# Rotary embedding on one core: batch 0 in four parts, a fixed ring order, tables on ScalarE's queue

## Chip, cores and metric

The kernel runs on one core of a Trainium2 chip. The metric is the device time of one execution in microseconds (us), as the median of several runs. A core has five engines with an instruction stream each. Here VectorE (DVE) does the arithmetic, ScalarE (ACT) changes types, GpSimd (POOL) and SyncE (SP) issue DMA transfers, and TensorE (PE) does nothing. The transfers themselves are carried out by sixteen DMA engines, which serve all queues.

## The reference

```python
# x: (8, 2048, 16, 64) float32; cos, sin: (2048, 32) float32
x1 = x[..., :32]
x2 = x[..., 32:]
cos = cos[None, :, None, :]
sin = sin[None, :, None, :]
out1 = x1 * cos - x2 * sin
out2 = x1 * sin + x2 * cos
return np.concatenate([out1, out2], axis=-1)   # float32
```

Each of 8 batches has 2048 positions with 16 heads of 64 values. The two halves of a head are rotated against each other by the position's angle. A batch is 8.39 MB (8 MiB) in float32; all of x is read once and all of out is written once, 67.1 MB each way.

## The kernel before

**Tiling.** The 2048 positions of a batch lie on the 128 partitions, 16 successive positions on each (J = 16; the text calls them rows, index j). So a partition holds one run of 64 KB of x per batch. On the chip a batch is a float16 tile `xt` of 128 x 16384 values; a pool holds five of them (NBUF = 5). POOL's transfers change the type on the way: a load (L51) reads float32 and writes float16, a store (L58) does the reverse. SP's transfers don't change the type, so what SP moves goes through the float32 tile `head` (two rows) and is changed by ScalarE.

**Start.** SP issues three transfers, one behind the other on its queue: rows 0 to 2 of batch 0 into `head` (L36), the sine table (L45) and the cosine table (L46), 256 KB each. POOL issues the loads of batches 0 to 4, batch 0 without its first two rows. ScalarE turns `head` into the first rows of tile 0 (L75), and the tables into float16: `sin_h` (L79), `neg_h`, which is minus sine (L80), and `cos_h` (L81).

**A batch.** `rotate` is four VectorE instructions on a whole tile: v's first halves are x2 times `neg_h` (L67), v's second halves are x1 times `sin_h` (L68), xt is multiplied by `cos_h` in place (L70), and v is added to xt (L72). L67 and L68 take 8192 elements per partition, L70 and L72 take 16384. Then the tile is stored. When tile b has been stored, its buffer takes the load of batch b + 5.

**Order.** Each engine works through its own instructions in order, and POOL's transfers run in the order in which they were issued (the ring). A tile scheduler may move instructions of an engine; POOL's order came out as loads 0 to 4, stores 0 and 1, loads 5 and 6, stores 2 and 3, load 7, stores 4 to 6, then the two parts of the last store. A load into a used buffer waits until the store out of it has landed.

**End.** Batch 7 is stored in three parts: rows 0 to 9 (L95) and 9 to 14 (L97) by POOL, in this order by a dependency written out by hand; rows 14 to 16 are widened to float32 by ScalarE into `head` (L105) and sent by SP (L106), which waits, again by hand, until the part of L95 has landed.

Of the kernel before, what the change touches and what calls it, by code (L numbers as in the profile page):

```python
# [1 line left out]

# [4 lines left out]


@with_exitstack  # L10
def kernel(
    ctx: ExitStack,
    tc: tile.TileContext,
    x: bass.AP,
    cos: bass.AP,
    sin: bass.AP,
    out: bass.AP,
):
    nc = tc.nc
    f16 = mybir.dt.float16  # L20
    f32 = mybir.dt.float32

    B, S, H, D = x.shape
    Dh = D // 2
    P = nc.NUM_PARTITIONS
    J = S // P
    NBUF = 5

    const_pool = ctx.enter_context(tc.tile_pool(name="rope_const", bufs=1))
    io_pool = ctx.enter_context(tc.tile_pool(name="rope_io", bufs=NBUF))  # L30
    tmp_pool = ctx.enter_context(tc.tile_pool(name="rope_tmp", bufs=1))

    JA = 2
    head = const_pool.tile([P, JA, H, D], f32)
    x0 = x[0].rearrange("(p j) h d -> p j (h d)", j=J)
    nc.sync.dma_start(  # L36
        out=head.rearrange("p j h d -> p (j h d)"),
        in_=x0[:, 0:JA, :].rearrange("p j f -> p (j f)"),
    )
    sin_f = const_pool.tile([P, J, Dh], f32)  # L40
    cos_f = const_pool.tile([P, J, Dh], f32)
    cos_h = const_pool.tile([P, J, Dh], f16)
    sin_h = const_pool.tile([P, J, Dh], f16)
    neg_h = const_pool.tile([P, J, Dh], f16)
    nc.sync.dma_start(out=sin_f, in_=sin.rearrange("(p j) d -> p j d", j=J))  # L45
    nc.sync.dma_start(out=cos_f, in_=cos.rearrange("(p j) d -> p j d", j=J))  # L46

    def load(b):
        xt = io_pool.tile([P, J, H, D], f16)
        j0 = JA if b == 0 else 0  # L50
        nc.gpsimd.dma_start(  # L51
            out=xt[:, j0:J, :, :].rearrange("p j h d -> p (j h d)"),
            in_=x[b].rearrange("(p j) h d -> p j (h d)", j=J)[:, j0:J, :].rearrange("p j f -> p (j f)"),
        )
        return xt

    def store(b, xt):
        nc.gpsimd.dma_start(  # L58
            out=out[b].rearrange("(p j) h d -> p (j h d)", j=J), in_=xt
        )  # L60

    def rotate(xt):
        v = tmp_pool.tile([P, J, H, D], f16)
        sin_b = sin_h.unsqueeze(2).to_broadcast([P, J, H, Dh])
        neg_b = neg_h.unsqueeze(2).to_broadcast([P, J, H, Dh])
        cos_b = cos_h.unsqueeze(2).to_broadcast([P, J, 2 * H, Dh])
        nc.vector.tensor_mul(out=v[:, :, :, 0:Dh], in0=xt[:, :, :, Dh:D], in1=neg_b)  # L67
        nc.vector.tensor_mul(out=v[:, :, :, Dh:D], in0=xt[:, :, :, 0:Dh], in1=sin_b)  # L68
        xw = xt.rearrange("p j h (e d) -> p j (h e) d", d=Dh)
        nc.vector.tensor_mul(out=xw, in0=xw, in1=cos_b)  # L70
        xa = xt.rearrange("p j h d -> p (j h d)")
        nc.vector.tensor_add(out=xa, in0=xa, in1=v.rearrange("p j h d -> p (j h d)"))  # L72

    tiles = [load(b) for b in range(NBUF)]
    nc.scalar.copy(  # L75
        out=tiles[0][:, 0:JA, :, :].rearrange("p j h d -> p (j h d)"),
        in_=head.rearrange("p j h d -> p (j h d)"),
    )
    nc.scalar.copy(out=sin_h, in_=sin_f)  # L79
    nc.scalar.mul(out=neg_h, in_=sin_f, mul=-1.0)  # L80
    nc.scalar.copy(out=cos_h, in_=cos_f)  # L81
    def part(b, j0, j1):
        return (
            out[b].rearrange("(p j) h d -> p j (h d)", j=J)[:, j0:j1, :].rearrange("p j f -> p (j f)"),
            tiles[b][:, j0:j1, :, :].rearrange("p j h d -> p (j h d)"),
        )

    for b in range(B):
        rotate(tiles[b])
        if b < B - 1:  # L90
            store(b, tiles[b])
        if b + NBUF < B:
            tiles.append(load(b + NBUF))
    dst, src = part(B - 1, 0, 9)
    gate = nc.gpsimd.dma_start(out=dst, in_=src)  # L95
    dst, src = part(B - 1, 9, J - JA)
    rest = nc.gpsimd.dma_start(out=dst, in_=src)  # L97
    tc.add_manual_dep(
        rest.ins,
        gate.ins.name,  # L100
        mybir.DependencyInfo(mybir.DependencyClass.NoSync, mybir.DependencyReason.DATA),
        reason="order of the ring",
    )
    dst, src = part(B - 1, J - JA, J)
    nc.scalar.copy(out=head.rearrange("p j h d -> p (j h d)"), in_=src)  # L105
    end = nc.sync.dma_start(out=dst, in_=head.rearrange("p j h d -> p (j h d)"))  # L106
    tc.add_manual_dep(
        end.ins,
        gate.ins.name,
        mybir.DependencyInfo(mybir.DependencyClass.Sync, mybir.DependencyReason.DATA),  # L110
        reason="the last rows go out behind this part",
    )


# [1 line left out]
_INS = ['x', 'cos', 'sin']  # L116
_OUTS = [((8, 2048, 16, 64), 'float32')]


# [23 lines left out]
```

## Time and profile before

| what | value |
|---|---|
| median of 3 runs | 317.42 us (317.40 to 317.48) |
| the profiled execution, its own time | 317.42 us |
| its span (first to last instruction in the trace) | 315.6 us |
| VectorE | 32 instructions |
| `rotate` of one batch, four instructions | 4.43 + 4.42 + 8.69 + 8.69 us |
| ScalarE | 6 instructions, 6.8 us |
| POOL, one DMA issue | 0.53 to 0.67 us of POOL's time |
| load 0 from issue to landing | 22.2 us |
| sin, cos from issue to landing | 15.2 us, 33.9 us |
| `head` in, from issue to landing | 4.7 us |
| `head` out, from issue to landing | 8.4 us |
| first VectorE instruction | starts at 23.51 us |
| last VectorE instruction | starts at 254.99 us, 8.69 us long |

How to read it: all times count from the start of the span. The time of a DMA issue on POOL's or SP's stream is the time of issuing, not of moving data; a landing is the semaphore that tells that all data have arrived. "DMA share" is the mean busy share of the sixteen DMA engines in a stretch; packets are counted where they are recorded, so a short stretch can show a share over 1. The bytes of a transfer that changes type are counted in the type of its destination, so a load of x at full pace shows about half the GB/s of a store.

### The profile page before, as it was taken

Reading aid. Unit: us, or ns where it says so; the run is one execution under the profiler, and the core shown is the slowest. Engines: PE = TensorE matmul, PEld = TensorE weight load, DVE = VectorE, ACT = ScalarE, POOL = GpSimd, SP = SyncE. Lnnn points to the kernel's source line nnn. Section 1 sums busy time; section 2 is a strip of 40 time slices with the busy share of each in tenths; the row PEclk is TensorE's granted clock in tenths of the full one; section 3 lists DMA queues with packets and bytes.
Section 4 is the critical chain, followed back from the end, with each engine's and each line's share of the span. In section 5 each row is a group of like instructions: output and inputs, shape, how many; then the busy total and the mean of one; then the engine's idle time right before and its main releaser. Section 6 shows DMA issues by size and latency. Waiting matters only on the chain.

```text
span 315.6 us, 126 instructions
## 1 busy us (share of the span) xinstructions
DVE 209.2 (66%) x32; ACT 6.8 (2%) x6; POOL 9.4 (3%) x21
## 2 busy tenths in 40 slices
DVE  0009599999999999999979999990009994000000
ACT  4010000000000000000000000000000002000000
POOL 3000000000000000010000000100000001000000
DMA  9899999999999999999999999999999999999998
GB/s 278 184 261 207 200 249 216 199 199 249 216 199 266 399 424 507 399 332 233 233 199 199 390 407 399 399 532 266 199 224 507 399 399 498 432 399 399 432 424 341
DMA packets 3024, 101.71 MB, mean 322 GB/s; under 512 B 336, under 2 KB 336, under 8 KB 592
## 3 DMA queue, kind: packets, MB, share of 16 engines
q0 software_dynamic: 2448, 99.09, 98.0%
q1 hardware_dynamic: 576, 2.62, 2.2%
HBM read 67.63 MB, written 67.11 MB: 427 GB/s over the span
## 4 chain that ended last, share of the span: by engine, by line
issue 25%; DMA 23%; DVE 21%; another core or an unknown queue 13%; POOL 1%; ACT 1%; SPq 0%; POOLq 0%; DVEq 0%; ACTq 0%
DMA xt<-in_x_dram 12%; DMA cos_f<-in_cos_dram 11%; DVE xt L70 8%; DVE xt L72 8%; DVE v L68 3%; DVE v L67 1%; ACT head L105 1%; POOL out_dram L58 1%; POOL xt L51 0%; ACT cos_h L81 0%; SPq L45 0%; SPq L36 0%; POOLq L58 0%; DVEq L67 0%
## 5 line engine op out<-in xcount | busy, mean ns | idle before, releaser
L70 DVE TENSOR_TENSOR xt<-xt,cos_h 128x16384 f16<-128x16384 f16 x8 | 69.5, 8692 | 4.2 <-ACT cos_h L81 3.9
L72 DVE TENSOR_TENSOR xt<-xt,v 128x16384 f16<-128x16384 f16 x8 | 69.5, 8692 | 0.3
L67 DVE TENSOR_TENSOR v<-xt,neg_h 128x8192 f16<-128x8192 f16 x8 | 35.4, 4425 | 50.1 <-DMA xt<-in_x_dram 49.9
L68 DVE TENSOR_TENSOR v<-xt,sin_h 128x8192 f16<-128x8192 f16 x8 | 35.3, 4417 | 0.0
L51 POOL DMA_DIRECT2D xt<-in_x_dram x8 | 4.4, 560 | 117.1 <-DMA out_dram<-xt 116.3
L105 ACT CAST head<-xt 128x2048 f32<-128x2048 f16 x1 | 1.9, 1897 | 227.6 <-DVE xt L72 227.6
L58 POOL DMA_DIRECT2D out_dram<-xt x7 | 3.7, 535 | 87.8 <-DVE xt L72 87.8
L95 POOL DMA_DIRECT2D out_dram<-xt x1 | 0.5, 531 | 50.5 <-DVE xt L72 50.5
L75 ACT CAST xt<-head 128x2048 f16<-128x2048 f32 x1 | 1.9, 1898 | 3.4 <-DMA head<-in_x_dram 3.4
L75 ACT ACT_TABLE_LOAD x1 | 1.3, 1283 | 0.7 <-PEq L127 0.7
L81 ACT CAST cos_h<-cos_f 128x512 f16<-128x512 f32 x1 | 0.6, 617 | 18.0 <-DMA cos_f<-in_cos_dram 18.0
L79 ACT CAST sin_h<-sin_f 128x512 f16<-128x512 f32 x1 | 0.6, 617 | 9.1 <-DMA sin_f<-in_sin_dram 9.1
L80 ACT ACTIVATE neg_h<-sin_f 128x512 f16<-128x512 f32 x1 | 0.6, 624 | 0.0
L97 POOL DMA_DIRECT2D out_dram<-xt x1 | 0.5, 531 | 0.0
L127 POOL MEMSET const-float32-0.0<- 128x1 f32 x1 | 0.1, 98 | 0.2 <-issue 0.2
L127 POOL MEMSET const-bfloat16-1.0<- 128x1 bf16 x1 | 0.1, 101 | 0.0
L127 POOL MEMSET const-float32-1.0<- 128x1 f32 x1 | 0.1, 98 | 0.0
L127 POOL MEMSET const-uint8-127<- 128x1 uint8 x1 | 0.1, 98 | 0.0
## 6 DMA issues: line engine op xcount, KB each, us to landing
xt<-in_x_dram POOLq DMA_DIRECT2D x7, 4096.0 KB, 41.1
out_dram<-xt POOLq DMA_DIRECT2D x1, 4608.0 KB, 42.3
xt<-in_x_dram POOLq DMA_DIRECT2D x1, 3584.0 KB, 22.2
out_dram<-xt POOLq DMA_DIRECT2D x1, 2560.0 KB, 47.9
head<-in_x_dram SPq DMA_DIRECT2D x1, 1024.0 KB, 4.7
out_dram<-head SPq DMA_DIRECT2D x1, 1024.0 KB, 8.4
sin_f<-in_sin_dram SPq DMA_DIRECT2D x1, 256.0 KB, 15.2
cos_f<-in_cos_dram SPq DMA_DIRECT2D x1, 256.0 KB, 33.9
```

Of the source, the lines that this page charges most:

```text
L51: nc.gpsimd.dma_start(out=xt[:, j0:J, :, :].rearrange("p j h d -> p (j h d)"), in_=x[b].rearrange("(p j) h d -> p j (h d)", j=J)[:, j0:J, ...
L58: nc.gpsimd.dma_start(out=out[b].rearrange("(p j) h d -> p (j h d)", j=J), in_=xt)
L67: nc.vector.tensor_mul(out=v[:, :, :, 0:Dh], in0=xt[:, :, :, Dh:D], in1=neg_b)
L68: nc.vector.tensor_mul(out=v[:, :, :, Dh:D], in0=xt[:, :, :, 0:Dh], in1=sin_b)
L70: nc.vector.tensor_mul(out=xw, in0=xw, in1=cos_b)
L72: nc.vector.tensor_add(out=xa, in0=xa, in1=v.rearrange("p j h d -> p (j h d)"))
L75: nc.scalar.copy(out=tiles[0][:, 0:JA, :, :].rearrange("p j h d -> p (j h d)"), in_=head.rearrange("p j h d -> p (j h d)"),)
L79: nc.scalar.copy(out=sin_h, in_=sin_f)
L80: nc.scalar.mul(out=neg_h, in_=sin_f, mul=-1.0)
L81: nc.scalar.copy(out=cos_h, in_=cos_f)
L95: gate = nc.gpsimd.dma_start(out=dst, in_=src)
L105: nc.scalar.copy(out=head.rearrange("p j h d -> p (j h d)"), in_=src)
```

## The change

The two rows of the last batch no longer take their own way; batch 7 is stored whole by POOL. Instead batch 0 is cut at rows 2, 6 and 10. Its first two rows still come through `head`, and its other rows are loaded in three POOL transfers; each of the four parts is rotated by four VectorE instructions of its own and stored when done, the first part through ScalarE, `head` and SP, the others by POOL. The sine and cosine tables are issued from ScalarE's queue rather than from SP's. Every POOL transfer of the ring is tied to the one before it, so that POOL issues them in the order in which they are written: load 0 in three parts, store of rows 2 to 6, store of rows 6 to 10, load 1, store of rows 10 to 16, loads 2 and 3, store 1, load 4, store 2, load 5, and so on, with load 7 behind store 4 and stores 5, 6 and 7 at the end. In the built program ScalarE first issues the two tables, then makes `sin_h` and `neg_h`, then the first rows of tile 0, then `cos_h`, then widens the rotated first rows. VectorE has 44 instructions on data in place of 32.

```diff
-    nc.sync.dma_start(out=head..., in_=x0[:, 0:JA, :]...)
...
-    nc.sync.dma_start(out=sin_f, in_=sin.rearrange("(p j) d -> p j d", j=J))
-    nc.sync.dma_start(out=cos_f, in_=cos.rearrange("(p j) d -> p j d", j=J))
+    cuts = [JA, 6, 10, J]
...
+    nc.sync.dma_start(out=flat(head), in_=rows(x, 0, 0, JA))
+    nc.scalar.dma_start(out=sin_f, in_=sin.rearrange("(p j) d -> p j d", j=J))
+    nc.scalar.dma_start(out=cos_f, in_=cos.rearrange("(p j) d -> p j d", j=J))
+
+    last = []
+
+    def ring(dma):
+        if last:
+            tc.add_manual_dep(
+                dma.ins,
+                last[-1].ins.name,
+                mybir.DependencyInfo(mybir.DependencyClass.NoSync, mybir.DependencyReason.DATA),
+                reason="order of the ring",
+            )
+        last.append(dma)
+
+    def load(b, j0, j1):
+        ring(nc.gpsimd.dma_start(out=flat(tiles[b][:, j0:j1, :, :]), in_=rows(x, b, j0, j1)))
+
+    def store(b, j0, j1):
+        ring(nc.gpsimd.dma_start(out=rows(out, b, j0, j1), in_=flat(tiles[b][:, j0:j1, :, :])))
+
+    def rotate(b, j0, j1):
+        xt = tiles[b]
+        n = j1 - j0
+        js = slice(j0, j1)
+        vt = tmp_pool.tile([P, J, H, D], f16)
+        v = vt[:, 0:n, :, :]
...
+        nc.vector.tensor_mul(out=v[:, :, :, 0:Dh], in0=xt[:, js, :, Dh:D], in1=neg_b)
+        nc.vector.tensor_mul(out=v[:, :, :, Dh:D], in0=xt[:, js, :, 0:Dh], in1=sin_b)
+        xw = xt[:, js, :, :].rearrange("p j h (e d) -> p j (h e) d", d=Dh)
+        nc.vector.tensor_mul(out=xw, in0=xw, in1=cos_b)
+        xa = flat(xt[:, js, :, :])
+        nc.vector.tensor_add(out=xa, in0=xa, in1=flat(v))
...
+    fresh(0)
+    for j0, j1 in zip(cuts, cuts[1:]):
+        load(0, j0, j1)
+    nc.scalar.copy(out=flat(tiles[0][:, 0:JA, :, :]), in_=flat(head))
     nc.scalar.copy(out=sin_h, in_=sin_f)
     nc.scalar.mul(out=neg_h, in_=sin_f, mul=-1.0)
     nc.scalar.copy(out=cos_h, in_=cos_f)
...
-    for b in range(B):
-        rotate(tiles[b])
-        if b < B - 1:
-            store(b, tiles[b])
-        if b + NBUF < B:
-            tiles.append(load(b + NBUF))
...
-    nc.scalar.copy(out=head.rearrange("p j h d -> p (j h d)"), in_=src)
-    end = nc.sync.dma_start(out=dst, in_=head.rearrange("p j h d -> p (j h d)"))
...
+    rotate(0, 0, JA)
+    nc.scalar.copy(out=flat(head), in_=flat(tiles[0][:, 0:JA, :, :]))
+    nc.sync.dma_start(out=rows(out, 0, 0, JA), in_=flat(head))
+    rotate(0, cuts[0], cuts[1])
+    store(0, cuts[0], cuts[1])
+    rotate(0, cuts[1], cuts[2])
+    store(0, cuts[1], cuts[2])
+    fresh(1)
+    load(1, 0, J)
+    rotate(0, cuts[2], cuts[3])
+    store(0, cuts[2], cuts[3])
+    fresh(2)
+    load(2, 0, J)
+    fresh(3)
+    load(3, 0, J)
+    for b in range(1, B):
+        rotate(b, 0, J)
+        store(b, 0, J)
+        if b + 3 < B:
+            fresh(b + 3)
+            load(b + 3, 0, J)
```

`fresh(b)` takes a new tile from the pool of five for batch b; `rows` and `flat` are the access patterns of a transfer's two sides, as before.

More of the change, by code (lines that the diff above doesn't have):

```diff
@@ L33 @@
     JA = 2
[L34 to L39, printed above, removed]
+    cuts = [JA, 6, 10, J]
     sin_f = const_pool.tile([P, J, Dh], f32)
@@ L44 @@
     neg_h = const_pool.tile([P, J, Dh], f16)
-    nc.sync.dma_start(out=sin_f, in_=sin.rearrange("(p j) d -> p j d", j=J))
-    nc.sync.dma_start(out=cos_f, in_=cos.rearrange("(p j) d -> p j d", j=J))
-    def load(b):
-        xt = io_pool.tile([P, J, H, D], f16)
[L50 to L78, printed above, removed]
+    head = const_pool.tile([P, JA, H, D], f32)
+    def flat(t):
+        return t.rearrange("p j h d -> p (j h d)")
+    def rows(t, b, j0, j1):
+        return t[b].rearrange("(p j) h d -> p j (h d)", j=J)[:, j0:j1, :].rearrange("p j f -> p (j f)")
+    nc.sync.dma_start(out=flat(head), in_=rows(x, 0, 0, JA))
@@ new lines, in store @@
+    def store(b, j0, j1):
[6 more added lines that the diff above has]
+        v = vt[:, 0:n, :, :]
+        sin_b = sin_h[:, js, :].unsqueeze(2).to_broadcast([P, n, H, Dh])
+        neg_b = neg_h[:, js, :].unsqueeze(2).to_broadcast([P, n, H, Dh])
+        cos_b = cos_h[:, js, :].unsqueeze(2).to_broadcast([P, n, 2 * H, Dh])
+        nc.vector.tensor_mul(out=v[:, :, :, 0:Dh], in0=xt[:, js, :, Dh:D], in1=neg_b)
[4 more added lines that the diff above has]
+        nc.vector.tensor_add(out=xa, in0=xa, in1=flat(v))
@@ L79, with fresh @@
+    tiles = {}
+    def fresh(b):
+        xt = io_pool.tile([P, J, H, D], f16)
+        tiles[b] = xt
+    fresh(0)
+    for j0, j1 in zip(cuts, cuts[1:]):
+        load(0, j0, j1)
+    nc.scalar.copy(out=flat(tiles[0][:, 0:JA, :, :]), in_=flat(head))
     nc.scalar.copy(out=sin_h, in_=sin_f)
@@ L81 @@
     nc.scalar.copy(out=cos_h, in_=cos_f)
[L82 to L86, printed above, removed]
-    for b in range(B):
-        rotate(tiles[b])
-        if b < B - 1:
-            store(b, tiles[b])
-        if b + NBUF < B:
-            tiles.append(load(b + NBUF))
[L94 to L104, printed above, removed]
-    nc.scalar.copy(out=head.rearrange("p j h d -> p (j h d)"), in_=src)
[L106 to L112, printed above, removed]
+    rotate(0, 0, JA)
[19 more added lines that the diff above has]
+            load(b + 3, 0, J)
 _INS = ['x', 'cos', 'sin']
```

## The prediction, made before the changed kernel was run

> **What bounds the kernel now.** I read the page's busy table and its forty slices first, then its DMA queues, then stretches of the span, then the instructions in order of time. Page, engines and queues:
>
> ```profile
> span 315.6 us, 126 instructions
> DVE 209.2 (66%) x32; ACT 6.8 (2%) x6; POOL 9.4 (3%) x21
> ...
> DMA  9899999999999999999999999999999999999998
> ...
> DMA packets 3024, 101.71 MB, mean 322 GB/s; under 512 B 336, under 2 KB 336, under 8 KB 592
> q0 software_dynamic: 2448, 99.09, 98.0%
> q1 hardware_dynamic: 576, 2.62, 2.2%
> HBM read 67.63 MB, written 67.11 MB: 427 GB/s over the span
> ```
>
> VectorE works for two thirds of the span; the sixteen DMA engines never fall below eight tenths, and the POOL queue (q0) alone fills 98.0%. So the DMA engines are the bound, and a change is worth what it does to their idle time, nothing else. The packet counts say how a transfer looks: 2448 = 17 POOL transfers x (128 + 16), so one packet for each partition row, eight on each engine, and one completion packet per engine; q1 likewise is 4 x 144.
>
> In order of time (start, duration, instruction), only the starting and ending lines and those of POOL that were held back by a store:
>
> ```profile
> 0.74 0.38 SPq L36 DMA_DIRECT2D head<-in_x_dram  x1
> 1.17 0.43 SPq L45 DMA_DIRECT2D sin_f<-in_sin_dram  x1
> 1.25 2.79 POOL L51 DMA_DIRECT2D xt<-in_x_dram  x5 [0.80 <-PEq L138]
> ...
> 5.45 1.90 ACT L75 CAST xt<-head 128x2048 f16<-128x2048 f32 x1 [3.43 <-DMA head<-in_x_dram]
> 16.41 0.62 ACT L79 CAST sin_h<-sin_f 128x512 f16<-128x512 f32 x1 [9.07 <-DMA sin_f<-in_sin_dram]
> ...
> 23.51 4.43 DVE L67 TENSOR_TENSOR v<-xt,neg_h 128x8192 f16<-128x8192 f16 x1 [23.51 <-DMA xt<-in_x_dram]
> ...
> 35.55 0.62 ACT L81 CAST cos_h<-cos_f 128x512 f16<-128x512 f32 x1 [17.98 <-DMA cos_f<-in_cos_dram]
> ...
> 54.18 0.54 POOL L58 DMA_DIRECT2D out_dram<-xt  x1 [50.14 <-DVE xt L72]
> ...
> 121.83 0.53 POOL L51 DMA_DIRECT2D xt<-in_x_dram  x1 [41.14 <-DMA out_dram<-xt]
> ...
> 141.13 0.53 POOL L51 DMA_DIRECT2D xt<-in_x_dram  x1 [18.76 <-DMA out_dram<-xt]
> ...
> 306.36 0.35 SPq L106 DMA_DIRECT2D out_dram<-head  x1
> ```
>
> Three things are to be seen. The stores of batches 0 and 1 landed 19.30 us apart (121.83 to 141.13): that is the pace of one batch on a full ring, 1.21 us for each of the 16 rows per partition (j), and 2.41 us for one 64 KB packet. The cosine table, 256 KB, landed at 35.5; batch 0 could not be finished before, and its store was issued at 54.18. Nobody paid for that: five loads were queued at the start and kept the ring full to about 102 (121.8 less one store). All this cover is what the new order gives up.
>
> **The change, part by part.** The time before is one execution: span 315.65 us (three decimals 315.649), its run 317.42, so 1.77 lies around the span; 317.42 is also the median of the three runs.
>
> *Ring order.* POOL now issues: batch 0 in three loads (rows 2 to 6, 6 to 10, 10 to 16; I call them La, Lb, Lc), store of rows 2 to 6 (Sa), store of rows 6 to 10 (Sb), load 1, store of rows 10 to 16, loads 2 and 3, and from there store b, load b+3. Sa waits for VectorE, and since the order is fixed, Sb, load 1 and everything else stands behind that wait. Loads 1 to 4 no longer cover the start: the ring holds 14/16 of a batch, the head, the tables and the small SP store until Sa, and nothing after Sa until Sb.
>
> *When the tables come.* sin landed at 16.4 and cos 19.1 us later, while POOL packets of 2.13 us (batch 0, 14 rows: 14/16 x 2.43) and 2.43 us ran; eight rows and a completion in 19.1 us is 2.12 us each. So while the ring is busy one small packet gets through for each big one. La and Lb have packets of four rows, 4 x 0.151 = 0.60 us. The head takes eight packets of 0.31 us per engine, the trace's packet records say, from 1.74; sin, now on a queue of its own, alternates with it (0.08 us each), so when POOL's first packet comes, at 5.10 in those records, some seven of eight are through on the slowest engine. Left are one sin packet and its completion, eight of cos and its completion: 11 turns of 0.60 + 0.09 = 7.6, so 12.7, and with the landing 12.9 for the start of the ACT cast. Bounds: 11 (one or two turns saved by completion packets, or HW packets passing together) and 15 (POOL's first packet at 3 to 4 instead of 5.1, as three issues now end at 3.0 where five ended at 4.04: every earlier POOL packet takes a turn from head and sin).
>
> The Trainium skill speaks against the queue move: "DMA: Bandwidth & Descriptors", section "Issuing engines are not separate DMA queues", says that transfers issued from several engines run on the same sixteen engines and that only issue time is saved. The row above does show one pool being shared; with the tables behind the head on SP's queue the count of turns after 5.1 would be the same 11 or so, so by the rule and by the row cos comes near 13: what shortens its wait is the size of the load packets.
>
> *VectorE's chain to Sb.* cast of cos 0.62 (L81's duration). A batch takes 26.24 us (53.65 to 79.89); the durations 4.424 for 8192 and 8.692 for 16384 elements give 1.92 elements per ns and about 0.64 us of start costs per batch, so 2 rows take 3.8, of which the last two instructions, after cos, 2.5; 4 rows take 25.6/4 + 0.64 = 7.04; 6 rows 10.2. Rows 0 to 2 end at 12.9 + 0.65 + 2.5 = 16.05, rows 2 to 6 at 23.1, rows 6 to 10 at 30.1. POOL starts 0.28 to 0.57 later (the gaps at 80.15 and 54.18), so Sa is issued at 23.5, Sb at 30.5, load 1 half a microsecond later. The ScalarE cast of rows 0 to 2 (1.90) ends at 18.0 and SP sends them at once.
>
> *What the DMA engines have until then.* Head, tables and batch 0 are through at about 23.5 (VectorE started on batch 0 at 23.51 before, four cos packets of 0.1 still open). The SP store adds 2.41, so 25.9; Sa adds 4 x 1.21 = 4.83, so 30.7. Beyond this the engines stand idle until Sb's first packet: 30.5 + latency.
>
> *Latency from a POOL issue to its first packet on an empty ring.* The trace has it once: issue at 1.25, first packet at 5.10, 3.85 us, cold and with four more issues behind it, and these stretches agree (columns: stretch, length, busy times, clock, DMA share, GB/s):
>
> ```profile
> 0.00:1.50 1.50, 0.00 (x0) 0.76 (x1) 0.46 (x5) 1.00 0.00 0
> 1.50:2.50 1.00, 0.00 (x0) 0.52 (x1) 1.00 (x3) 1.00 0.78 156
> 2.50:5.00 2.50, 0.00 (x0) 0.00 (x0) 1.54 (x3) 1.00 0.95 392
> ...
> 311.50:314.50 3.00, 0.00 (x0) 0.00 (x0) 0.00 (x0) 1.00 0.85 350
> 314.50:315.60 1.10, 0.00 (x0) 0.00 (x0) 0.00 (x0) 1.00 0.00 0
> ```
>
> 156 x 1.0 + 392 x 2.5 is 1.14 MB by 5.0: the head (1.05) and some sin, no load. The other end is SP's 1.0 us (issue 0.74, first packet 1.74); from the end of the fifth issue at 4.04 to 5.10 is also 1.06. I take 2.2, between the two readings of POOL's own row. Idle: 30.5 + 2.2 - 30.7 = **2.0 us**, from 0 (11 for cos, 1.0) to 5.7 (15, 3.85).
>
> The Trainium skill, "DMA: Bandwidth & Descriptors", section "Specifications", gives the first byte of the POOL path as about 1 us; by it the idle time would be 0.8 and the run near 317.9. No run here shows that figure on a warm queue.
>
> *Later waits.* VectorE needs 26.2 per batch, the ring 38.6 per load and store. Load 1 ends near 57, so store 1 is issued near 83 while loads 2 and 3 run to about 103; load 7 ends near 258, store 7 is issued near 284 while stores 5 and 6 run to 296. Load b+3 waits for store b-2, two transfers back. Cost nothing; without that cover a late store would cost what it is late.
>
> *Reads in a row.* Five loads, head and tables before took from 1.74 to about 101.9. At pace they are 5 x 19.3 (head included) + 1.4 of tables = 97.9, +0.45 for slow first packets; 1.2 us over is spread on loads 3 and 4 (packets of 2.5, and 3.3 for the last), while load and store pace elsewhere is 19.3. The new order has at most two loads in a row. If the row of five causes it, it goes; if it is the first touch of the output, most of it stays: -0.6, from -1.2 to 0.
>
> *The end.* The two rows that SP sent (eight packets of 0.31 = 2.47) go back into store 7 (2.41): nothing. A POOL landing is told about 0.2 us later than an SP landing (0.4 to 0.6 after the last packet against 0.3 to 0.4): +0.2. Three more transfers, 0.03 us each by the parts of the last store (10.89 for 9/16, at pace 10.86): +0.1. The removed ScalarE cast was hidden under stores.
>
> Sum: 2.0 - 0.6 + 0.3 = +1.7: span 317.35, time **319.1**.
>
> **The rivals.**
> 1. *The ring never runs dry.* If cos start plus latency is at most 13.1 (12.1 and 1.0, say), Sb arrives before Sa is done. Then -0.6 + 0.3 is left: 317.1, from 316.5 to 317.7. For it: the 1.06 us row, and the small packets; against it: VectorE needs 7.04 for a part that the DMA engines store in 4.83.
> 2. *Starved harder.* Latency 3.85 on every dry issue and cos at 15 give 5.7 + 0.3 - 0.6: 322.8; from 321.1 to 325. For it the only POOL row; against, that row is the first of the program.
> 3. *The tables come no sooner.* If POOL packets shut them out until batch 0 is loaded, cos comes at 23.5, 10.6 later: near 330. Against: sin and cos did get through, one per packet.
>
> **How the numbers follow.** Forecast 58% (idle 0.9 to 4.0: 318.1 to 321.1), rival 1 25%, rival 2 12%, rival 3 5%. 0.2% (0.63 us) is about what a measurement of this kernel can tell from no change: slower than 318.05 is 0.58 + 0.12 + 0.05 = 0.75. Rival 1 straddles 316.79: 0.15 within, 0.10 faster. The range leaves out about a tenth on each side: 316.8 to 321.8; the likeliest case's own is 318.1 to 321.1.
>
> **What would show it.** Cos cast at 11 to 15; POOL's Sa near 23.5 and Sb near 30.5, both released by VectorE; DMA shares well under 0.9 somewhere between 25 and 34, worth about 2 us, and none after; store 7 issued more than 10 us ahead of its turn. I am wrong if no stretch around 30 is below 0.9 (rival 1), if cos comes after 16, or if later stretches lose DMA time.

## The result and the profile after

The changed kernel takes 318.76 us (median of 6 runs, 318.42 to 319.39), the kernel before in the same comparison 317.45 us. The ratio is 1.0042, with a 95% interval of 1.0029 to 1.0055: slower by 1.3 us. The profiled execution took 318.73 us with a span of 316.95 (before: 317.42 and 315.65), so it shows the whole difference.

Page of the changed kernel, engines, slices and queues:

```profile
span 317.0 us, 145 instructions
DVE 210.8 (67%) x44; ACT 6.7 (2%) x6; POOL 11.1 (3%) x24
...
DMA  7999999999999999999999999999999999999996
...
q0 software_dynamic: 2880, 99.09, 97.8%
q1 hardware_dynamic: 288, 2.10, 1.8%
q10 hardware_dynamic: 288, 0.52, 0.5%
```

The tables have a queue of their own (q10). The slices that matter are not where the forecast looked: a dry ring around 30 us would lie in the fourth slice, and that is a 9. The last slice fell, from 8 to 6. The first fell too, from 9 to 7, but that is counting: a packet counts where its record stands, and the kernel before, with packets of 2.13 us at that place, shows a share of 1.37 for 5 to 10 us (1.06 now, with packets of 0.62), while 0 to 5 us show 0.63 and 0.64.

Instructions of the changed kernel in order of time:

```profile
7.22 0.62 ACT L96 CAST sin_h<-sin_f 128x512 f16<-128x512 f32 x1 [4.29 <-DMA sin_f<-in_sin_dram]
...
12.65 0.62 ACT L98 CAST cos_h<-cos_f 128x512 f16<-128x512 f32 x1 [2.49 <-DMA cos_f<-in_cos_dram]
...
23.12 0.54 POOL L68 DMA_DIRECT2D out_dram<-xt  x1 [20.14 <-DVE xt L84]
...
30.17 0.54 POOL L68 DMA_DIRECT2D out_dram<-xt  x1 [6.50 <-DVE xt L84]
30.69 0.54 POOL L65 DMA_DIRECT2D xt<-in_x_dram  x1
...
283.65 0.53 POOL L68 DMA_DIRECT2D out_dram<-xt  x1 [38.13 <-DVE xt L84]
```

The cosine cast at 12.65 and the stores Sa and Sb at 23.12 and 30.17 are within 0.4 us of the working (12.9, 23.5, 30.5), and store 7 was issued at 283.65 (284). So VectorE's chain is as worked out. But no DMA time was lost on Sb: in the trace's packet records Sa's last packets on the sixteen engines end from 31.39 to 32.04, and Sb's first packet starts at 31.39. The stretches agree:

```profile
27.00:31.00 4.00, 3.93 (x3) 0.00 (x0) 0.83 (x2) 1.00 1.09 446
31.00:32.00 1.00, 1.00 (x2) 0.00 (x0) 0.23 (x1) 1.00 0.95 377
32.00:37.00 5.00, 4.93 (x3) 0.00 (x0) 0.00 (x0) 1.00 1.40 475
```

The ring never ran dry there. From load 1 on, every transfer starts 19.32 us per batch after the one before it, to the end. Counted to the last data packet the changed kernel is only 0.25 us behind, 314.68 against 314.43.

The rest lies behind the last packet. There each engine drains (a DRAIN is an instruction that ends when the engine's own work is through, as VectorE's of 8725 ns does beside its last instruction of 8.69 us) and then takes part in the closing barrier, semaphores by which the engines tell one another that they are done. Two answers about the program's last line, first the kernel before, then the changed kernel (columns: engine's queue, operation, count, duration in ns as least/median/most, first and last start in us; POOL's longest drain is the one that starts first):

```profile
L138 POOLq EVENT_SEMAPHORE  x4: 17/17/17, 315.0 to 315.5; - x4
L138 POOLq DRAIN  x3: 39/95/48711, 264.4 to 315.4; - x3
...
L138 DVEq DRAIN  x2: 19/4372/8725, 255.0 to 315.2; - x2
```

```profile
L145 POOLq EVENT_SEMAPHORE  x4: 17/17/17, 315.9 to 316.8; - x4
L145 POOLq DRAIN  x3: 39/95/32267, 283.6 to 316.4; - x3
...
L145 DVEq DRAIN  x2: 143/4434/8725, 274.7 to 316.6; - x2
```

Before, POOL's drain ended at 264.4 + 48.7 = 313.1, while SP's last transfer was still running; that transfer landed at 314.78 (its last semaphore step in the trace) and POOL opened the closing barrier at 314.96, 0.17 later. In the changed kernel store 7 landed at 315.04, but POOL's drain ended only at 283.63 + 32.27 = 315.90 and the barrier opened at 315.94: 0.90 after the landing, so 0.73 us more. POOL's drain was as late before (its own last landing was at 312.35, the drain over 0.74 later, 0.86 in the changed kernel); SP's transfer ran meanwhile. Then VectorE's last drain came late (143 ns in place of 19, started at 316.59): from the barrier to the end it took 1.01 us in place of 0.69. The sum is 0.25 + 0.73 + 0.32 = 1.30 us, the difference of the spans.

### The profile page after: what moved, and what is told of

It is laid out like the page before. It is cut to its first block, busy times and chain, and to the rows that moved or that the text cites. A ratio compares the mean times of both kernels' runs of the same rounds, so it can differ in the third digit from the quotient of the medians.

```text
span 317.0 us, 145 instructions
## 1 busy us (share of the span) xinstructions
DVE 210.8 (67%) x44; ACT 6.7 (2%) x6; POOL 11.1 (3%) x24
## 5 line engine op out<-in xcount | busy, mean ns | idle before, releaser
L79 DVE TENSOR_TENSOR vt<-xt,neg_h 128x8192 f16<-128x8192 f16 (+3 forms) x11 | 35.9, 3261 | 70.0 <-DMA xt<-in_x_dram 59.7
L82 DVE TENSOR_TENSOR xt<-xt,cos_h 128x16384 f16<-128x16384 f16 (+3 forms) x11 | 70.0, 6364 | 2.2 <-ACT cos_h L98 1.8
L84 DVE TENSOR_TENSOR xt<-xt,vt 128x16384 f16<-128x16384 f16 (+3 forms) x11 | 70.0, 6365 | 0.4
L80 DVE TENSOR_TENSOR vt<-xt,sin_h 128x8192 f16<-128x8192 f16 (+3 forms) x11 | 35.8, 3253 | 0.0
L68 POOL DMA_DIRECT2D out_dram<-xt x10 | 5.4, 538 | 272.1 <-DVE xt L84 272.1
L65 POOL DMA_DIRECT2D xt<-in_x_dram x10 | 5.5, 558 | 0.8 <-PEq L145 0.8
## 6 DMA issues: line engine op xcount, KB each, us to landing
out_dram<-xt POOLq DMA_DIRECT2D x1, 3072.0 KB, 23.5
xt<-in_x_dram POOLq DMA_DIRECT2D x1, 1536.0 KB, 23.6
```

Source lines behind the costliest of these rows:

```text
L65: ring(nc.gpsimd.dma_start(out=flat(tiles[b][:, j0:j1, :, :]), in_=rows(x, b, j0, j1)))
L68: ring(nc.gpsimd.dma_start(out=rows(out, b, j0, j1), in_=flat(tiles[b][:, j0:j1, :, :])))
L79: nc.vector.tensor_mul(out=v[:, :, :, 0:Dh], in0=xt[:, js, :, Dh:D], in1=neg_b)
L80: nc.vector.tensor_mul(out=v[:, :, :, Dh:D], in0=xt[:, js, :, 0:Dh], in1=sin_b)
L84: nc.vector.tensor_add(out=xa, in0=xa, in1=flat(v))
```

## The experiments

The kernel before ran beside each of them; the ratio is to it. Its median was 317.34 in the first comparison, and 317.40, 317.44 and 317.64 in the next three, so ratios are to be compared rather than times.

**1. The old ending on the changed kernel.** Edit, in place of the whole store of batch 7:

```diff
-        store(b, 0, J)
+        if b < B - 1:
+            store(b, 0, J)
...
+    store(B - 1, 0, 9)
+    gate = last[-1]
+    store(B - 1, 9, J - JA)
+    nc.scalar.copy(out=flat(head), in_=flat(tiles[B - 1][:, J - JA:J, :, :]))
+    end = nc.sync.dma_start(out=rows(out, B - 1, J - JA, J), in_=flat(head))
```

(with SP's transfer behind `gate` as before).

> The changed kernel with the ending of the kernel before (rows 14 to 16 of batch 7 through ScalarE and SP, rows 0 to 14 in two POOL parts). Theory A, the loss sits in the end: in the changed kernel the last landing is at 315.04, POOL's drain lets go only at 315.94 and the span ends at 316.95; before, landing 314.78, POOL 314.96, end 315.65. With SP's transfer last POOL is drained early, so some 0.7 us come back: 318.0 (317.8 to 318.3). Rival B, the loss is idle DMA time at the start, as forecast: the end changes nothing, 318.8 (318.6 to 319.0).

Measured: 317.81 us, ratio 1.0015 (1.0006 to 1.0024), against 1.0042 without it. Two lines about its last program line:

```profile
L157 POOLq DRAIN  x3: 39/93/29502, 284.0 to 315.6; - x3
...
L157 DVEq DRAIN  x2: 142/4434/8727, 274.6 to 315.8; - x2
```

POOL's drain is over at 313.5, and the barrier opens at 315.16, 0.17 after the landing at 314.99. VectorE's late drain stays, and with it 0.3 us. Theory A. (POOL's own last landing is at 312.56, so its drain is over 0.90 later, hidden as in the kernel before.)

**2. The new ending on the kernel before.** The three parts of the last store replaced by one:

```diff
-        if b < B - 1:
-            store(b, tiles[b])
+        store(b, tiles[b])
```

> The kernel before with batch 7 stored whole by POOL and nothing else changed. Theory A: POOL's drain comes after the last landing here too: 0.7 to 1.1 us more, 318.1 to 318.6. Rival B: the end costs at most the 0.2 us of the prediction: 317.4 to 317.7.

Measured: 317.89, ratio 1.0016 (1.0007 to 1.0025), 0.55 us more: theory A in kind, a little less than its range. The drain here ends at 264.0 + 51.45 = 315.45, the barrier opens at 315.50, 0.74 after the last landing at 314.76, and VectorE is not late.

```profile
L118 POOLq DRAIN  x3: 39/95/51446, 264.0 to 315.9; - x3
...
L118 DVEq DRAIN  x2: 19/4372/8725, 255.1 to 315.7; - x2
```

**3. The tables back on SP's queue.** In the changed kernel `nc.sync.dma_start` in place of `nc.scalar.dma_start` for both tables.

> The changed kernel with the two tables back on SP's queue, behind the head. Theory A, small load packets and not the queue brought cos forward, one table packet for each load packet: cos cast at 12 to 13.5, the ring stays full, 318.8 (318.5 to 319.0). Rival C, the own queue brought it forward: cos cast at 15 or later, store of rows 6 to 10 issued after 32.5, ring dry, 320 or more.

Measured: 320.10, ratio 1.0082 (1.0068 to 1.0096). My theory A fell. From its instructions in order of time, and its DMA stretches:

```profile
9.23 0.62 ACT L96 CAST sin_h<-sin_f 128x512 f16<-128x512 f32 x1 [1.64 <-DMA sin_f<-in_sin_dram]
...
14.83 0.62 ACT L98 CAST cos_h<-cos_f 128x512 f16<-128x512 f32 x1 [4.46 <-DMA cos_f<-in_cos_dram]
...
32.36 0.54 POOL L68 DMA_DIRECT2D out_dram<-xt  x1 [6.51 <-DVE xt L84]
```

```profile
27.00:31.00 4.00, 3.93 (x3) 0.00 (x0) 0.00 (x0) 1.00 1.10 451
31.00:32.00 1.00, 1.00 (x1) 0.00 (x0) 0.00 (x0) 1.00 0.16 49
32.00:33.50 1.50, 1.47 (x2) 0.00 (x0) 1.07 (x2) 1.00 0.18 76
33.50:37.00 3.50, 3.46 (x3) 0.00 (x0) 0.00 (x0) 1.00 1.02 417
```

cos came 2.18 us later (14.83 against 12.65), Sb with it, and the ring was dry from 31.86, the end of Sa's last packet, to 33.46, Sb's first: 1.6 us. (A packet is counted where its record stands, so the share of 1.10 ahead of the hole includes work done in it.) Here is the dry ring of the forecast, in a kernel that it was not made for. The rule of the Trainium skill, "DMA: Bandwidth & Descriptors", section "Issuing engines are not separate DMA queues", that issue from several engines saves only issue time, does not hold in this place: the issue of cos came 0.47 us sooner on ScalarE's queue (1.16 against 1.63), its landing 2.18. One pool of DMA engines is shared, but the packet records show the queues taking turns on it, packet by packet; apart from these turns a table waits only behind what stands on its own queue. When POOL's first packet started, 114 of the 256 table packets had started in the changed kernel and 58 here, so 3.5 turns fewer were left on each engine; at 0.70 us (one load packet and one table packet) that makes an estimated 2.4 us.

**4. A part that comes too late.** Cuts at 2, 6 and 12 in the changed kernel:

```diff
-    cuts = [JA, 6, 10, J]
+    cuts = [JA, 6, 12, J]
```

> The changed kernel with batch 0 cut at 2, 6 and 12, so that VectorE needs 10.2 us for the part that the ring waits for: it is issued at about 33.4 and the ring is dry from about 31.4. This shows the time from a POOL issue to the first packet on a dry, warm queue. If it is about 1 us, the DMA engines idle for 3.0 us and the run takes 321.8 (321.4 to 322.2); with the 2.2 us of the prediction 323.0; with the 3.85 us of the first load 324.6.

Measured: 321.60, ratio 1.0133 (1.0119 to 1.0147). Issue and stretches:

```profile
33.67 0.54 POOL L68 DMA_DIRECT2D out_dram<-xt  x1 [9.71 <-DVE xt L84]
```

```profile
31.00:32.00 1.00, 1.00 (x1) 0.00 (x0) 0.00 (x0) 1.00 0.24 82
32.00:34.50 2.50, 2.47 (x2) 0.00 (x0) 0.83 (x2) 1.00 0.00 0
34.50:38.00 3.50, 3.47 (x3) 0.00 (x0) 0.24 (x1) 1.00 1.07 449
```

The first packet after the hole is at 34.77, 1.10 us after the issue at 33.67; in experiment 3 it was 33.46 - 32.36 = 1.10 too. That is the latency of a POOL transfer on an empty ring once the program runs (1.11 in experiments 8 and 10 as well); the 3.85 us of the first load do not recur. Of the three expectations it is the first, about 1 us.

**5. A small early write to the output.** The kernel before, with 64 bytes per partition written at the start from ScalarE's queue:

```diff
+    mark = const_pool.tile([P, 16], f32)
+    nc.vector.memset(mark, 0.0)
+    nc.scalar.dma_start(
+        out=out[0].rearrange("(p j) h d -> p (j h d)", j=J)[:, 0:16], in_=mark
+    )
```

> The kernel before with one more transfer at the start: ScalarE's queue writes 64 bytes of each partition's first output run (zeros, overwritten later by store 0). In the kernel before the last packets of load 4, right ahead of the first store, take 3.2 to 3.4 us instead of 2.43, and load 4 takes 20.37 us instead of 19.32; in the changed kernel the loads beside the first small store are slowed alike, 0.98 us over. Theory A, the first write to the output costs it: load 4 goes back to about 19.4 and the run takes 316.4 to 317.0, or stays at 317.3 if the stall moves to the start. Rival B, it belongs to the first large store: load 4 stays at 20.4, 317.3.

Measured: 317.36, ratio 0.9996 (0.9987 to 1.0005). The last packets of load 4 still take 2.8 to 3.56 us and load 4 takes 19.95, between the two expectations (19.4 and 20.4). But with the same ring order and no touch it takes 20.08 and 19.93 (experiments 6 and 7, below), so this is rival B: the small touch leaves the slowing of the last loads where it was, and that the first write to the output as such makes them slow is out.

**6 and 7. More VectorE instructions.** The kernel before with twelve, then fifteen, one-element memsets at its start:

```diff
+    mark = const_pool.tile([P, 16], f32)
+    for i in range(12):      # 15 in the second
+        nc.vector.memset(mark[:, i:i + 1], 0.0)
```

> The kernel before with twelve VectorE memsets of one element per partition at the start, when VectorE is idle, so that it has 44 instructions as the changed kernel has. At the end of the changed kernel and of the one with the old ending VectorE's last drain takes 0.14 us instead of 0.02 and comes 0.4 us later after the barrier. Theory A, it goes with the number of VectorE instructions: late drain here too, 317.6 to 317.7. Rival B, it has another cause: drain of 0.02 us, 317.3 to 317.4.

> The kernel before with fifteen one-element memsets on VectorE instead of twelve: counted with the waits and branches that the trace holds, VectorE then has 65 instructions like the changed kernel (the run with twelve had 62 and a drain of 0.02 us). Theory A, a count between 62 and 65 makes the last drain late: 0.14 us, 0.4 us after the barrier, 317.7. Rival B, no such count: 317.4.

Measured: 317.44, ratio 1.0000 (0.9991 to 1.0009) with twelve, 317.67, ratio 1.0007 (0.9999 to 1.0016) with fifteen. The times alone leave the second open; the trace does not. With twelve (rival B), then with fifteen (theory A):

```profile
L142 DVEq DRAIN  x2: 19/4372/8725, 255.0 to 315.2; - x2
```

```profile
L142 DVEq DRAIN  x2: 143/4434/8725, 255.0 to 315.5; - x2
```

In all twelve kernels VectorE's late drain goes with the number of records of its stream in the trace, waits and branches included: 50 to 64 (the kernel before, experiments 2, 5, 6, 8, 9 and 10) without it, 65 (the changed kernel, experiments 1, 3, 4 and 7) with it. Why the count matters the runs don't show.

**8. No SP store at the start.** In the changed kernel rows 0 to 2 go out with rows 2 to 6:

```diff
-    nc.scalar.copy(out=flat(head), in_=flat(tiles[0][:, 0:JA, :, :]))
-    nc.sync.dma_start(out=rows(out, 0, 0, JA), in_=flat(head))
     rotate(0, cuts[0], cuts[1])
-    store(0, cuts[0], cuts[1])
+    store(0, 0, cuts[1])
```

> The changed kernel with rows 0 to 2 of batch 0 stored by POOL together with rows 2 to 6, without the ScalarE cast and the SP store. Batch 0 is then loaded at about 23.1 with nothing behind it until the first store, issued at 23.1 and, with 1.1 us latency, started at 24.2: 1.1 us of idle at this place, and the next part (issued 30.2, ready 31.3) in time before the 7.25 us store ends at 31.5. Theory A, the 0.98 us that the last loads beside the SP store lost in the changed kernel come from running beside it: the loads end undisturbed at 23.1, load 1 starts near 36.3 as it did, 318.7 (318.4 to 318.9). Rival B, the first store costs about 1 us wherever it stands: load 1 starts at 37.3, 319.6.

Measured: 317.98, ratio 1.0014 (1.0005 to 1.0023): faster than expected by 0.7. The loads of batch 0 ran undisturbed, every packet of the third part in 0.93 us (0.93 to 1.69 in the changed kernel), the ring was dry for 0.4 to 1.0 us on the single engines until the first store's packets at 24.24, and load 1 started at 36.36 (36.25), as theory A had it. What I had not counted is that the DMA engines then run in step: the first packets of a store start within 0.16 us of each other on the sixteen engines, in the changed kernel within 0.69, and that spread is carried to the last packet (314.26 against 314.68). The other 0.3 is VectorE's drain, which with 64 records is short here.

**9 and 10. A version that takes the best of it.** Experiment 8 with the old ending; in experiment 9 with cuts at 2, 5 and 8 besides, so that the first stores come in time:

```diff
-    cuts = [JA, 6, 10, J]
+    cuts = [JA, 5, 8, J]      # experiment 9 only
```

> The kernel without the SP store at the start (rows 0 to 5 by POOL as the first store), with batch 0 cut at 2, 5 and 8 and with the old ending. VectorE then needs 5.44 us, not 7.04, for each of the two parts that the ring waits for: first store issued at about 21.5, ready at 22.6 while the loads run to 23.2; second issued at 27.0, ready at 28.1 while the first runs to 29.2. No idle time is left at the start (1.0 us less), and the old ending takes 0.5 to 0.7 us off: from the 317.98 of the run without the SP store, 316.3 to 316.6, faster than both kernels. If the end of the loads is again slowed by a store that starts while they run (the 0.98 us), or if the DMA engines come out of step again (0.4 us), 316.8 to 317.4.

> The same with the cuts of the changed kernel (2, 6 and 10): only the ending differs from the run without the SP store. 0.5 to 0.7 us from POOL's late drain come back: 317.3 to 317.5, about the kernel before.

Measured: 317.30, ratio 0.9985 (0.9976 to 0.9994), for experiment 9, which fell into the worse of its two branches; 317.12, ratio 0.9976 (0.9966 to 0.9986), for experiment 10, below its expectation. In both the ratio to the kernel before is under 1, by 0.5 and 0.8 us. But in this comparison the kernel before took 317.64; against its 317.34 to 317.44 beside the other experiments experiment 9 gains nothing clear and experiment 10 some 0.2 to 0.3 us, so a gain is not firmly shown. In experiment 9 the first store was queued at 19.95, while the loads ran to between 23.6 and 24.4, and again the last load packets were slow, 1.6 to 2.0 us in place of 1.23, and the engines out of step by 0.78. In experiment 10 the first store found an empty ring, the loads were even and the spread was 0.15. The ring was dry there for 0.4 to 0.7 us, and yet the last data packet ended at 313.91, in experiment 9 at 314.38. The medians are only 0.18 us apart and the intervals overlap, so that the dry ring was the cheaper of the two is what the two profiled executions show, and no more.

## Why the prediction was right, and where it was not

The time (319.1 forecast, 318.76 measured), the sign and VectorE's chain were right. The mechanism was not, and that the sum came so near is luck: idle time was 0 in place of 2.0, reads in a row +0.25 in place of -0.6, the end +1.05 in place of +0.3. All three terms were off, and the errors nearly cancelled. The forecast's own sign of being wrong, no stretch around 30 below 0.9, is what the profile shows.

- *Tables and VectorE's chain.* Right to 0.4 us (12.65, 23.12, 30.17). The argument that the queue did not matter was wrong: I counted the same 11 turns for both queues. Experiment 3 puts the own queue at 2.2 us sooner and, with the ring at its limit, at 1.3 us of run time. On a queue of its own sin alternates with the head; behind it, 3.5 more table packets for each engine are left when POOL's packets come.
- *Latency on an empty ring.* This is the step that failed: I took 2.2 us and idle time of 2.0. It is 1.10 (experiments 3 and 4), near the lower end that I had named, and the ring was just covered: rival 1 in its mechanism. The cover was narrow. Sb was ready at 30.17 + 1.10 = 31.27, Sa was through at 31.39 on the first engine. The latency alone would not have covered it: against the 30.7 of the working 0.6 us of idle time would have been left, and the next term took that away.
- *What the DMA engines have until then.* I had Sa's end at 30.7; it was 31.4 at the earliest, because the last loads beside the SP store were slowed by 0.98 us in all (15.84 to 26.53, at pace 7.24 + 2.47). Experiment 8, without the SP store, has none of it.
- *Reads in a row.* Forecast -0.6. The 0.35 us of slower packets on loads 3 and 4 did not recur; but they are no price of five loads in a row, for experiments 5, 6 and 7, with the same row, run load 3 at pace (19.32). They belong to the one execution that was read. The larger piece, slow last packets ahead of the first store, was kept in another place (0.85 us before, packets of 3.28 on the mean in place of 2.43; 0.98 after), and a wider spread over the DMA engines was added (0.69 against 0.39). To the last packet the balance is +0.25. (The working's 97.9 + 0.45 + 1.2 is also 0.6 short of the 100.2 us that it was to explain.)
- *The end.* Another mis-sized term, and the larger part of the loss: +0.3 forecast, +1.05 measured in the profile. Landings were told equally fast (0.36 after the last packet in both kernels); I had not looked at what runs after the last landing. SP's last transfer, whose removal I costed at nothing, hid POOL's drain (0.73), and VectorE's late drain came on top (0.32). Experiments 1 and 2, the ending put back and the ending alone, give 0.27% (0.85 us) and 0.16% (0.5 us) for it.
- *Later waits.* Right: no transfer after load 1 was late.

## What to carry to other kernels

When the DMA engines are busy throughout, look at what stands after the last packet: POOL's queue, whose drain was 0.7 to 0.9 us late here, is better not the one that carries the last transfer. Put small tables on a queue of their own when large packets share the engines, because queues take turns packet by packet (2.2 us here). And a full ring is not the aim in itself: a first store queued behind running loads slowed them and put the engines out of step, in the profiled executions at a higher price than half a microsecond of dry ring.

## What was not expected of the hardware

- POOL's drain lets go 0.7 to 0.9 us after the landing of POOL's last transfer: 315.90 against 315.04 (changed kernel), 315.45 against 314.76 (experiment 2), 313.09 against 312.35 (the kernel before, hidden behind SP).
- VectorE's last drain takes 0.14 instead of 0.02 us, and the end comes 0.3 us later in the profile, from some count of instructions on (64 records without, 65 with).
- The last loads ahead of the first store of the program are slow when that store is already queued (2.8 to 3.6 us in place of 2.43 in the kernel before and experiment 5; 1.6 to 2.0 in place of 1.23 in experiment 9) and not when it comes to an empty ring (experiments 8 and 10). Later changes from loads to stores cost nothing: 19.32 us each. A touch of the output does not cure it; its cause stays open.
